# Gates and branch projections with rows stationary, and merged rows transposed for the output projection

## The chip, the core and the metric

The kernel runs on one core of a Trainium2 chip. The core has a matrix engine (TensorE, PE in the profile; its weight loads are PEld), a vector engine (VectorE, DVE), an activation engine (ScalarE, ACT), GpSimd (POOL), and SyncE (SP), which here issues the DMA transfers. SBUF is the working memory with 128 partitions; matmul results land in PSUM, which has eight banks of 128 x 512 float32 here. The metric is the device time of one execution in microseconds; lower is better.

A matmul has a stationary operand (loaded into the array as weights, 128 x 128 here) and a moving operand (128 x N columns that stream through it). The result has the stationary operand's columns on the partitions and the moving operand's columns along the row.

## The reference, cut to what matters

Two layers. Each has a token-mixing sub-layer with two attention branches, merged by gates, and then an MLP. The sequence has 256 rows, the model width is 1024.

```python
for l in range(DEPTH):
    ada = c_act @ w_ada[l] + b_ada[l]
    sh1, sc1, gt1, sh2, sc2, gt2 = [a[:, None, :] for a in jnp.split(ada, 6, axis=-1)]
    h = rms(x, g_mix[l]) * (1.0 + sc1) + sh1
    parts = jnp.split(h @ w_in[l], IN_SPLITS, axis=-1)
...
    y_a = gqa_attention(qa, ka, va) @ w_branch_a[l]
...
    y_b = dilated_attention(qs, kss, vs) @ w_branch_b[l]
    gate_a = jax.nn.sigmoid(parts[3 + 3 * N_B])
    gate_b = jax.nn.sigmoid(parts[4 + 3 * N_B])
    mixed = gate_a * y_a + gate_b * y_b
    x = x + gt1 * (mixed @ w_out[l])
    h2 = rms(x, g_mlp[l]) * (1.0 + sc2) + sh2
    x = x + gt2 * (jnp.square(jax.nn.relu(h2 @ w_ff1[l])) @ w_ff2[l])
```

The change concerns `gate_a`, `gate_b`, `y_a`, `y_b` (the two branch projections) and `mixed`.

## The kernel before, in words

**Precision.** Every large matmul is done with operands split in two: `hi` is the value rounded to the matmul's float32 form and `lo` the remainder. `mm3` issues three matmuls into the same PSUM accumulation: hi x hi, lo x hi, hi x lo. Weights arrive from HBM as 128 x 1024 float32 tiles of 512 KB into one of six `wr` buffers; ACT copies the tile to `hi`, DVE subtracts to get `lo` (`split_next`, called through `weights` and `weights_k`). These two operations are the groups `w<-wr` of ACT and `w<-wr,w` of DVE.

**Layouts.** The normalised rows `h` are kept transposed: `hT` has the model width on partitions (8 tiles of 128) and the 256 rows along the free axis, as hi and lo. Attention outputs `oa` (4 tiles) and `ob` (2 tiles) are kept in the same way.

**Two ways of multiplying.** The q, k, v chunks (`qkv_chunk`) use a piece of `hT` (128 of its rows) as the stationary operand and move 512 weight columns: the result has rows on partitions. The gates, the projection of branch A (`ya`) and of branch B (the loop at the end of `mixer`, called yb below) go the other way, through `wide`: 128 weight columns are stationary and all 256 rows move, so that the result has model columns on partitions and rows along the free axis, one 128 x 256 half of a PSUM bank at a time. A unit of each fills one bank.

- `gates(l, hT, G, u, bank)`, eight units a layer: two weight tiles, 2 x 8 x 3 matmuls of 256 columns, then on ACT a tanh out of PSUM into `G` and a scale-and-shift in place (a sigmoid). `G[0]` is gate A, `G[1]` gate B.
- `ya`, four units: one weight tile, 2 x 4 x 3 matmuls, then one DVE multiply of the bank by gate A into `M`.
- yb, four units: 2 x 2 x 3 matmuls, a DVE multiply by gate B, a DVE add of `M`, then ACT copies the sum to `mT` hi and DVE subtracts for `mT` lo.

`mT` is therefore already transposed (model width on partitions), as the output projection needs it for its stationary operand. The output projection takes each of the two blocks of 128 rows (t = 0, 1) against 512 columns of `w_out` at a time: 2 x 2 x 8 x 3 matmuls. Its result goes through `residual` and `make_h` into the MLP. In the MLP `two_sums` multiplies with weights stationary and both halves of `h2` moving: one matmul of 512 and one of 256 columns per weight tile's block.

**Order.** Every operation is recorded by a helper (all have line 551 in the profile) and a planner decides the order on each engine before anything is issued: `Plan.run` is a list scheduler over the engines with costs of its own and due times, run four times (`PASSES`) with the best kept; the tiles of a pool get buffers in that order. The recorded sequence within a mixer is written by hand in `CFG["seq0"]` and `CFG["seq1"]`: `c3` a qkv chunk, `u` or `v` a gate unit, `a` a step of attention A, `b` a pair of heads of attention B, `y` a unit of `ya`, `w` one step of ada (a 512 KB tile of `w_ada` multiplied by the conditioning vector and summed along the row on DVE: the group `s2k<-wr,c_act`). PSUM tiles all come from one pool of eight banks (`pa`, `pb` and `pt` are the same).

Attention A's step: scores of two heads, maximum on DVE, exponentials on ACT, scaling by the reciprocal sum on ACT, transposes of the probabilities by TensorE, a copy to SBUF on ACT, and the product with v. Attention B's pair does the same on 128 x 512 tiles, with a masked pass on DVE in place of the maximum.

## Time and profile before

| | |
|---|---|
| device time, median of 3 runs | 755.84 us |
| lowest and highest run | 755.43 and 757.5 us |
| span of the profiled execution, first to last instruction | 754.0 us |
| TensorE busy | 739.9 us, 98% |
| TensorE weight loads busy | 629.9 us, 84% |
| VectorE busy | 595.4 us, 79% |
| ScalarE busy | 470.7 us, 62% |
| moved by DMA | 180.47 MB, mean 239 GB/s |

The profile is one execution. A row of a timeline gives start, length, engine, line, operation, the tiles written and read with their shapes, and a count; in brackets the idle time of the engine before it and what ended it. A row of a group gives the same shapes with a count, and behind the bars the busy time in us and the mean of one in ns, then the idle time before it. Tile names: `ps` a PSUM bank, `w` a split weight tile, `wr` a raw one, `s2k` a small work tile, `consts` the identity of the transposes, `pr` probabilities, `qk` and `ka` queries and keys, `st` the softmax statistics.

In layer 0 the mixer's gates and attention lie between about 66 and 171 us of the span, yb from 171.57, the output projection from 177.23, and the MLP's first matmul at 199.95. In layer 1 the mixer runs from about 386 us, yb starts at 538.22 and the output projection at 543.87.

### The profile page before, as it was taken

What the parts mean: (1) busy time and instruction counts of PE and PEld (TensorE: products, weight loads), DVE (VectorE), ACT (ScalarE), POOL (GpSimd) and SP (SyncE); (2) the same over time, 40 slices, a digit from 0 to 9 for tenths busy, and PEclk for the clock granted to TensorE, in tenths of its full rate; (3) what the DMA queues carried; (4) which work ended last, traced back from release to release, by engine and by line L of the source; (5) the groups of instructions that cost most, each with busy time, mean ns of one, the idle gap of its engine ahead of it and who ended that gap; (6) DMA issues with size and microseconds to landing.
All of it is one profiled execution on the core that took longest, in us unless ns stands there. A gap on an engine that the chain in (4) does not pass through costs nothing.

```text
span 754.0 us, 11447 instructions
## 1 busy us (share of the span) xinstructions
PE 739.9 (98%) x4246; PEld 629.9 (84%) x4246; DVE 595.4 (79%) x905; ACT 470.7 (62%) x784; POOL 70.2 (9%) x60
## 2 busy tenths in 40 slices
PE   7999999999999999999999999999998999999997
PEld 4888898998788888888888788889987888888886
DVE  5999999889899989566499899778879976556633
ACT  8668469785558766655256557599535865555630
POOL 0007840000000060000002111000000000000000
PEclk9999999999999999999999999999999999999999
DMA  8996379976579999666145566966635986656201
GB/s 336 385 401 208 128 246 330 356 261 234 178 283 370 386 355 341 248 223 222 58 155 182 219 242 236 363 198 212 235 140 184 344 305 224 204 191 219 88 29 56
DMA packets 50391, 180.47 MB, mean 239 GB/s; under 512 B 5624, under 2 KB 6048, under 8 KB 50336
## 3 DMA queue, kind: packets, MB, share of 16 engines
q1 hardware_dynamic: 50336, 179.75, 66.6%
q8 instruction: 33, 0.54, 0.3%
q14 instruction: 22, 0.18, 0.1%
HBM read 178.66 MB, written 1.06 MB: 238 GB/s over the span
## 4 chain that ended last, share of the span: by engine, by line
PE 84%; DVE 7%; issue 4%; ACT 3%; DMA 1%; POOL 1%; SPq 0%; POOLq 0%; ACTq 0%; DVEq 0%
PE ps L551 84%; DVE s2k L551 4%; DVE w L551 2%; ACT s2k L551 2%; DVE rstd L551 1%; DMA x<-in_x 1%; ACT pr L551 1%; ACT w L551 0%; POOL s2k L551 0%; DVE x L551 0%; DVE hT L551 0%; ACT xT L551 0%; SPq L551 0%; POOL ss L551 0%; ACT c_act L551 0%
## 5 line engine op out<-in xcount | busy, mean ns | idle before, releaser
L551 DVE TENSOR_TENSOR w<-wr,w 128x1024 fp32r<-128x1024 f32 x236 | 288.0, 1238 | 61.0 <-ACT w L551 60.6
L551 ACT ACTIVATE w<-wr 128x1024 fp32r<-128x1024 f32 x236 | 245.6, 1058 | 87.2 <-PE ps L551 48.0
L551 PE MATMUL ps<-hT,w 128*128 128x256 f32 (+1 forms) x1664 | 263.8, 315 | 0.0
L551 PEld LDWEIGHTS ps<-hT,w 128*128 128x128 f32 x1664 | 234.4, 190 | 23.6 <-issue 2.6
L551 PE MATMUL ps<-w,r2k 128*128 128x512 f32 (+1 forms) x792 | 178.8, 385 | 0.0
L551 PEld LDWEIGHTS ps<-w,r2k 128*128 128x128 f32 x792 | 144.4, 188 | 30.1
L551 PE MATMUL ps<-w,hT 128*128 128x512 f32 x672 | 163.3, 399 | 5.0 <-DVE hT L551 2.7
L551 PEld LDWEIGHTS ps<-w,hT 128*128 128x128 f32 x672 | 126.2, 191 | 33.8 <-DVE hT L551 4.5
L551 DVE CUSTOM_DVE_ANT_0 s2k<-wr,c_act 128x1024 bf16<-128x1024 f32 x96 | 117.7, 1240 | 2.3 <-DMA wr<-in_w_ada 1.6
L551 ACT ACTIVATE s2k<-ps 128x512 f32<-128x512 f32 (+3 forms) x136 | 61.5, 479 | 64.0 <-PE ps L551 55.0
L551 PE MATMUL ps<-w,mT 128*128 128x512 f32 x192 | 44.5, 391 | 0.0
L551 ACT ACTIVATE s2k<-s2k 128x512 f32<-128x512 f32 (+1 forms) x62 | 38.3, 620 | 6.0 <-DVE s2k L551 5.2
L551 PEld LDWEIGHTS ps<-w,mT 128*128 128x128 f32 x192 | 35.8, 188 | 7.3
L551 POOL TENSOR_TENSOR rstd<-rstd,half 128x8 f32<-128x8 f32 (+1 forms) x20 | 35.7, 1795 | 61.7 <-DVE rstd L551 61.7
L551 DVE TENSOR_TENSOR s2k<-ps,s2k 128x256 f32<-128x256 f32 x56 | 23.6, 421 | 17.1 <-ACT s2k L551 17.1
L551 ACT ACTIVATE pr<-pr,st 128x256 f32<-128x256 f32 (+1 forms) x64 | 35.7, 614 | 0.6 <-DVE st L551 0.6
L551 POOL TENSOR_TENSOR ss<-ss,half 128x1 f32<-128x1 f32 x8 | 4.4, 554 | 312.2 <-DVE ss L551 312.2
L551 DVE TENSOR_TENSOR r2k<-s2k,r2k 128x512 fp32r<-128x512 f32 x28 | 19.6, 699 | 15.6 <-ACT r2k L551 15.6
L551 ACT ACTIVATE s2k<-x 128x512 bf16<-128x512 f32 x16 | 10.0, 627 | 31.2 <-DVE x L551 28.3
L551 DVE TENSOR_TENSOR s2k<-ps,gtb 128x512 f32<-128x512 f32 (+1 forms) x18 | 11.8, 659 | 20.5 <-PE ps L551 18.7
L551 PE MATMUL ps<-oa,w 128*128 128x256 f32 x192 | 26.1, 288 | 0.0
L551 PE MATMUL ps<-consts,s2k 128*128 128x128 f32 x148 | 22.6, 281 | 2.9 <-DVE s2k L551 2.4
(82 smaller groups left out, 498.1 us busy)
## 6 DMA issues: line engine op xcount, KB each, us to landing
wr<-in_w_ff SPq DMA_DIRECT2D x120, 512.0 KB, 5.2
wr<-in_w_ada SPq DMA_DIRECT2D x96, 512.0 KB, 5.3
wr<-in_w_gate SPq DMA_DIRECT2D x32, 512.0 KB, 5.1
wr<-in_w_qkv SPq DMA_DIRECT2D x24, 512.0 KB, 4.6
wr<-in_w_x SPq DMA_DIRECT2D x16, 512.0 KB, 3.2
wr<-in_w_out SPq DMA_DIRECT2D x16, 512.0 KB, 5.4
wr<-in_w_y SPq DMA_DIRECT2D x8, 512.0 KB, 5.5
wr<-in_w_ba SPq DMA_DIRECT2D x8, 512.0 KB, 4.9
```

Source lines behind the costliest of these rows:

```text
L551: getattr(self.real[o["e"]], o["op"])(*map(real, o["a"]), **{n: real(z) for n, z in o["k"].items()})
```

## The change

The gates and `ya` now work as the qkv chunks do: 128 rows of `hT` or `oa` are stationary and 512 weight columns move. Two PSUM banks, one for each block of rows, are filled by four weight tiles (a gate group, two of the old units) or two (`ya`). `G` and `M` have rows on partitions. The gate weights and those of branch A are laid out on the host in tiles that fit (`w_gate`, `w_ba`); sizes and counts of the tiles stay.

yb too has rows stationary. Its merged result has rows on partitions, and TensorE transposes it, four 128 x 128 blocks into one PSUM bank, from which ACT and DVE make `mT` hi and lo for one block of rows. The loop goes over the blocks of rows first, then over the two column halves; both weight tiles of branch B are fetched ahead of it. `CFG`, with the two hand-written sequences, is unchanged; `u`, `v`, `y`, `z` no longer name a bank.

```diff
-    def gates(l, hT, G, u, bank):
-        if u % 4 == 0:
-            G.append(tl("sbuf", [P, 2048], F32, "b8", NB8, f"G{l}{u}"))
-        ps = bank(f"g{l}_{u}")
-        for i in range(2):
-            wh, wl = weights_k(KT)
-            wide(ps, i, wh, wl, hT, KT)
-
-        z = G[u // 4][:, (u % 4) * 512 : (u % 4 + 1) * 512]
-        act.activation(z, ps, AF.Tanh, scale=0.5)
-        act.activation(z, z, AF.Copy, scale=0.5, bias=0.5)
+    def gates(l, hT, G, pss, u):
+        g, part = divmod(u, 2)
+        if g % 2 == 0 and part == 0:
+            G.append(tl("sbuf", [P, 2, D], F32, "b8", NB8, f"G{l}{g}"))
+        if part == 0:
+            pss[:] = [pb(f"g{l}_{g}_{t}") for t in range(2)]
+        for j in (2 * part, 2 * part + 1):
+            wh, wl = weights_k(2)
+            for t in range(2):
+                for k in range(2):
+                    kk = 2 * j + k
+                    lh, ll = hT.parts(kk, slice(t * P, (t + 1) * P))
+                    mm3(pss[t], lh, ll, wh[:, k, :], wl[:, k, :], kk == 0, kk == KT - 1)
+        if part == 0:
+            return
+        for t in range(2):
+            z = G[g // 2][:, t, (g % 2) * 512 : (g % 2 + 1) * 512]
+            act.activation(z, pss[t], AF.Tanh, scale=0.5)
+            act.activation(z, z, AF.Copy, scale=0.5, bias=0.5)
...
-        def ya(u, bank):
-            wh, wl = weights_k(4)
-            ps = bank(f"ya{l}_{u}")
-            for i in range(2):
-                wide(ps, i, wh[:, :, i * P : (i + 1) * P], wl[:, :, i * P : (i + 1) * P], T["oa"], 4)
-            dve.tensor_tensor(
-                fl(M[:, 2 * u : 2 * u + 2, :]), ps, G[0][:, u * 512 : (u + 1) * 512], op=ALU.mult
-            )
+        def ya(y):
+            c, part = divmod(y, 2)
+            if part == 0:
+                yps[:] = [pa(f"ya{l}_{c}_{t}") for t in range(2)]
+            wh, wl = weights_k(2)
+            for t in range(2):
+                for k in range(2):
+                    kk = 2 * part + k
+                    lh, ll = T["oa"].parts(kk, slice(t * P, (t + 1) * P))
+                    mm3(yps[t], lh, ll, wh[:, k, :], wl[:, k, :], kk == 0, kk == 3)
+            if part == 1:
+                cs = slice(c * 512, (c + 1) * 512)
+                for t in range(2):
+                    dve.tensor_tensor(M[:, t, cs], yps[t], G[0][:, t, cs], op=ALU.mult)
...
-        for v in range(2):
-            wh, wl = weights_k(2)
-            for uu in range(2):
-                u = 2 * v + uu
-                ps = pa(f"yb{l}_{u}")
-                for i in range(2):
-                    n0 = (2 * uu + i) * P
-                    wide(ps, i, wh[:, :, n0 : n0 + P], wl[:, :, n0 : n0 + P], T["ob"], 2)
-                t = s2k(f"yb{l}_{u}s")
-                dve.tensor_tensor(t, ps, G[1][:, u * 512 : (u + 1) * 512], op=ALU.mult)
-                dve.tensor_tensor(t, t, fl(M[:, 2 * u : 2 * u + 2, :]), op=ALU.add)
-                hi, lo = (fl(z[:, 2 * u : 2 * u + 2, :]) for z in mT)
-                act.activation(hi, t, AF.Copy)
-                dve.tensor_tensor(lo, t, f32(hi), op=ALU.subtract)
+        wb = [weights_k(2) for _ in range(2)]
+        for t in range(2):
+            ts = slice(t * P, (t + 1) * P)
+            for c in range(2):
+                cs = slice(c * 512, (c + 1) * 512)
+                ps = pa(f"yb{l}_{t}{c}")
+                for k in range(2):
+                    lh, ll = T["ob"].parts(k, ts)
+                    mm3(ps, lh, ll, wb[c][0][:, k, :], wb[c][1][:, k, :], k == 0, k == 1)
+                m = s2k(f"yb{l}_{t}{c}s")
+                dve.tensor_tensor(m, ps, G[1][:, t, cs], op=ALU.mult)
+                dve.tensor_tensor(m, m, M[:, t, cs], op=ALU.add)
+                tp = pt(f"mT{l}_{t}{c}")
+                for k in range(4):
+                    pe.transpose(tp[:, k * P : (k + 1) * P], m[:, k * P : (k + 1) * P], ident)
+                tv = tp.rearrange("p (k n) -> p k n", k=4)
+                hi, lo = (z[:, 4 * c : 4 * c + 4, ts] for z in mT)
+                act.activation(hi, tv, AF.Copy)
+                dve.tensor_tensor(lo, tv, f32(hi), op=ALU.subtract)
...
-    r["w_gate"] = tiles(blocks(wi[:, :, GA:], P), 1, 8).reshape(2, 16, P, 1024)
+    r["w_gate"] = tiles(blocks(wi[:, :, GA:], 512), 4, 2).reshape(2, 16, P, 1024)
...
-    r["w_ba"] = tiles(blocks(wa, 256), 1, 4).reshape(2, 4, P, 1024)
+    r["w_ba"] = tiles(blocks(wa, 512), 2, 2).reshape(2, 4, P, 1024)
```

More of the change, by code (lines that the diff above doesn't have):

```diff
@@ L1086, in mixer @@
         mT = []
-        def ya(u, bank):
-            wh, wl = weights_k(4)
-            ps = bank(f"ya{l}_{u}")
-            for i in range(2):
-                wide(ps, i, wh[:, :, i * P : (i + 1) * P], wl[:, :, i * P : (i + 1) * P], T["oa"], 4)
-            dve.tensor_tensor(
-                fl(M[:, 2 * u : 2 * u + 2, :]), ps, G[0][:, u * 512 : (u + 1) * 512], op=ALU.mult
-            )
-        M = tl("sbuf", [P, KT, S], F32, "b8", NB8, f"M{l}")
+        def ya(y):
[12 more added lines that the diff above has]
+                    dve.tensor_tensor(M[:, t, cs], yps[t], G[0][:, t, cs], op=ALU.mult)
+        gps, yps = [], []
+        M = tl("sbuf", [P, 2, D], F32, "b8", NB8, f"M{l}")
         for j in seq:
@@ L1101, in mixer @@
             elif j in "uv":
-                gates(l, hT, G, u, pa if j == "u" else pb)
+                gates(l, hT, G, gps, u)
                 u += 1
@@ L1110, in mixer @@
             elif j in "yz":
-                ya(y, pa if j == "z" else pb)
+                ya(y)
                 y += 1
```

## The prediction

> **What bounds the kernel now.** First the head of the page, then its chain of work that ended last, then the stretches in which only one kind of matmul runs, then the busy time of each engine over each mixer.
>
> ```profile
> span 754.0 us, 11447 instructions
> PE 739.9 (98%) x4246; PEld 629.9 (84%) x4246; DVE 595.4 (79%) x905; ACT 470.7 (62%) x784; POOL 70.2 (9%) x60
> PEclk9999999999999999999999999999999999999999
> PE 84%; DVE 7%; issue 4%; ACT 3%; DMA 1%; POOL 1%; SPq 0%; POOLq 0%; ACTq 0%; DVEq 0%
> ```
>
> TensorE is busy in 98% of the span, at the full granted clock in every slice, and carries 84% of the chain. So a change pays by what it takes off the time that TensorE needs, and costs by every wait that it puts on TensorE. The busy time of one matmul overlaps that of the next, so I price matmuls by their pitch: first start of one group to first start of the next, over the count. The timeline of TensorE (start, length, what, count) has pure stretches:
>
> ```profile
> 162.93 5.92 PE L551 MATMUL ps<-hT,w 128*128 128x256 f32 x48
> 168.69 3.04 PE L551 MATMUL ps<-oa,w 128*128 128x256 f32 x24
> 171.57 5.82 PE L551 MATMUL ps<-ob,w 128*128 128x256 f32 x48
> 177.23 15.84 PE L551 MATMUL ps<-w,mT 128*128 128x512 f32 x69
> 192.91 1.03 PE L551 MATMUL ps<-consts,s2k 128*128 128x128 f32 x8
> 193.70 6.42 PE L551 MATMUL ps<-w,mT 128*128 128x512 f32 x27
> ...
> 443.97 11.11 PE L551 MATMUL ps<-w,hT 128*128 128x512 f32 x48
> 454.91 4.83 PE L551 MATMUL ps<-hT,w 128*128 128x256 f32 x39
> ```
>
> Weights stationary, 256 columns moving: gates (168.69 - 162.93)/48 = 120 ns, ya (171.57 - 168.69)/24 = 120 ns, yb (177.23 - 171.57)/48 = 118 ns. Rows stationary, 512 weight columns moving, the form that the change goes over to: (454.91 - 443.97)/48 = 228 ns for qkv, (192.91 - 177.23)/69 = 227 ns in the output projection. Two of the old do the work of one new: 240 against 228 ns.
>
> **Part 1, fewer and wider matmuls.** Per layer the old gates are 8 units x 2 x 8 x 3 = 384 matmuls of 256 columns, ya 96, yb 48; the new ones are half as many of 512. The groups by shape confirm it for ya and yb:
>
> ```profile
> L551 PE MATMUL ps<-hT,w 128*128 128x256 f32 x1216 | 230.2, 285 | 0.0
> L551 PE MATMUL ps<-oa,w 128*128 128x256 f32 x192 | 26.1, 288 | 0.0
> L551 PE MATMUL ps<-ob,w 128*128 128x256 f32 x96 | 11.6, 279 | 0.0
> L551 PE MATMUL ps<-hT,w 128*128 128x512 f32 x448 | 157.3, 394 | 0.0
> ```
>
> (Of the 1216, 448 belong to the MLP's two_sums, one for each of its 448 wide matmuls; 768 are gates.) Both layers: 960 x 120 + 96 x 118 = 126.5 us before, 528 x 228 = 120.4 us after: -6.1 us. Bounds: with the output projection's 227 ns it is -6.7; if the wide form in the gates ran no better per column than the narrow one, 240 ns, it is nothing. I take -6.1, since the nearest row has the same hT as stationary operand and weights moving.
>
> A sentence apart: the Trainium skill, "TensorE: Matmul & The Clock Gate", section "Back-to-back issue gap", gives an isolated warm gap of N / 2.4 + 2.5 ns, so 109 and 216 ns for 256 and 512 columns. By it a pair saves only 2.5 ns, 528 pairs 1.3 us, and that speaks against the change. The rows have 120 and 228, so the trace does not agree and I keep its 12 ns.
>
> **Part 2, the transposes that come in.** yb now lands with rows on partitions, so four 128x512 results per layer are each turned by four 128x128 transposes: 8 groups in all. The trace has the same groups of four inside gate matmuls:
>
> ```profile
> 99.83 5.17 PE L551 MATMUL ps<-hT,w 128*128 128x256 f32 x41
> 104.84 0.61 PE L551 MATMUL ps<-consts,s2k 128*128 128x128 f32 x4
> 105.21 5.76 PE L551 MATMUL ps<-hT,w 128*128 128x256 f32 x46
> ```
>
> The four take 105.21 - 104.84 = 0.37 us to the next start, and the 41 before them 5.01 us instead of 41 x 0.120 = 4.92, 0.09 more: 0.46 us a group, 3.7 us in all. The eight at 192.91 take 0.79 us with no such step, 0.40 a group, 3.2 us. I take 3.6 us. The sum so far is -6.1 + 3.6 = -2.5 us.
>
> **Part 3, the seam from yb to the output projection.** DVE does as many operations as before (multiply, add, and the subtraction for lo, each four times a layer), ACT the same four copies; both now read the transpose from PSUM.
>
> ```profile
> L551 DVE TENSOR_TENSOR s2k<-ps,G 128x512 f32<-128x512 f32 x8 | 5.5, 688 | 0.9 <-PE ps L551 0.9
> L551 DVE TENSOR_TENSOR s2k<-s2k,M 128x512 f32<-128x512 f32 x8 | 5.4, 689 | 0.1
> L551 ACT ACTIVATE mT<-s2k 128x512 fp32r<-128x512 f32 x8 | 5.0, 628 | 9.9 <-DVE s2k L551 9.9
> L551 DVE TENSOR_TENSOR w<-wr,w 128x1024 fp32r<-128x1024 f32 x236 | 288.0, 1238 | 61.0 <-ACT w L551 60.6
> ```
>
> Count from the first yb matmul. The first group of six ends at 6 x 0.228 = 1.4 us, plus about 0.2 for its end; multiply and add finish at 3.0. In the order of the changed kernel 15 matmuls stand ahead of the first transposes: 3.4 us, no wait. hi ends at 4.7, lo at 5.4, and the first matmul on mT is due after 24 matmuls and 8 transposes, at 6.4: covered by the other yb groups. The other half of the rows (t = 1) is needed only after the 48 matmuls of t = 0, 11 us later. The tight place is the last transpose of layer 0: on DVE, w_183's split stands between its multiply and its add, so the add ends at 7.5 + 1.24 + 0.7 = 9.4 and TensorE is there at 9.2. Behind it the whole output projection is queued; I count 0.3 us. In layer 1 the splits are ahead of it, and the same count leaves no wait. Bounds 0 and 1.2 (one more split in the way). No transfer moves: the two re-laid weight tensors arrive in the same number of 512 KB tiles.
>
> **Part 4, what the shorter matmuls were covering.** DVE is almost as full as TensorE in the mixer of layer 0, and ACT during attention B. Busy time by stretch (layer 0's mixer, its attention B, its output projection, layer 1's mixer):
>
> ```profile
> core 0: us, PE busy (x) PEld busy (x) DVE busy (x) ACT busy (x) POOL busy (x), PEclk, DMA share, GB/s
> 66.30:171.50 105.20, 104.02 (x812) 92.86 (x811) 97.56 (x164) 80.47 (x161) 32.04 (x23) 1.00 0.75 261
> 405.70:538.20 132.50, 130.93 (x928) 114.95 (x927) 110.70 (x188) 94.16 (x174) 12.57 (x8) 1.00 0.71 252
> ...
> 142.00:163.00 21.00, 21.00 (x203) 18.85 (x202) 18.63 (x44) 20.06 (x39) 0.00 (x0) 1.00 0.78 276
> 177.20:200.00 22.80, 22.80 (x107) 18.92 (x106) 21.80 (x33) 10.23 (x19) 0.56 (x1) 1.00 0.55 185
> ```
>
> In layer 0's mixer TensorE falls by 240 pairs x 12 ns = 2.9 us, to 101.1, against 97.6 of DVE, whose work stays. That is 3.5 us of room, and in attention B ACT has 20.06 of 21.00. The new form also keeps two PSUM banks open (one for each half of the rows) over four weight tiles of gates or two of ya, where the old kept one open over two or one; there are eight banks. In the changed order the second pair of heads of attention B starts its scores only after the first pair's last product with v; before, they stood in between (142.06 and 147.07 against 153.41):
>
> ```profile
> 142.06 2.02 PE L551 MATMUL ps<-qk 64*128 64x256 f32 x24
> ...
> 147.07 1.15 PE L551 MATMUL ps<-qk 64*128 64x256 f32 x12
> ...
> 153.41 1.96 PE L551 MATMUL ps<-s2k,v 128*64 128x256 f32 x24
> ```
>
> ```profile
> 143.99 0.72 ACT L551 ACTIVATE pr<-pr,st 128x512 f32<-128x512 f32 x1 [0.56 <-DVE st L551]
> ...
> 146.12 2.55 ACT L551 ACTIVATE pr<-pr,st 128x512 f32<-128x512 f32 x4
> ```
>
> ```profile
> L551 DVE CUSTOM_DVE_ANT_0 s2k<-wr,c_act 128x1024 bf16<-128x1024 f32 x96 | 117.7, 1240 | 2.3 <-DMA wr<-in_w_ada 1.6
> ...
> L551 DVE CUSTOM_DVE_ANT_0 pr<-ps,mask 128x512 f32<-128x512 f32 x16 | 10.4, 685 | 3.0 <-PE ps L551 2.8
> ```
>
> So the second pair's first transpose waits for its scores, a mask pass of 0.69 us that stands behind an ada product of 1.24 on DVE, two exponentials of 0.72 and a scaling of 0.64, with nine wide matmuls (2.1 us) as cover: about 2 us of wait. Counted through operation by operation with these durations, the stretch from the first score to yb comes to 28.9 us. Before it took 171.57 - 142.06 = 29.5, from which part 1 takes 72 pairs x 12 ns = 0.9. So 0.3 us of the wait is a net loss. Attention A of this layer is rearranged in the same way; I give it 0.9, three of its transposes left with 0.3 us each. Together +1.2 for layer 0, and nothing for layer 1, where DVE has 22 us of room. Bounds: nothing, and the 2.9 us of layer 0's gain with the 2 us on top, 4.9. A gain is excluded: no operation of DVE or ACT goes.
>
> **Sum.** -6.1 + 3.6 + 0.3 + 1.2 = -1.0 us on the span of 754.0: 753.0. The page has no time for the profiled execution but the span; the span lies 1.84 us below the median of the runs, 755.84, which I take for launch and end and leave as it is: 754.8 us. A difference under 0.3%, 2.3 us, cannot be told from no change here. So the forecast is "the same", a little to the fast side.
>
> **Rivals.**
>
> *All of it arrives (faster, chance 0.28).* No wait of parts 3 and 4 comes, and the row-wise gates, which need one half of the rows at a time, also fill gaps at the head of layer 1, where narrow gates needed both halves:
>
> ```profile
> 398.62 0.73 PE L551 MATMUL ps<-consts,s2k 128*128 128x128 f32 x5 [0.60 <-DVE s2k L551]
> ...
> 410.58 0.66 PE L551 MATMUL ps<-consts,s2k 128*128 128x128 f32 x4 [0.44 <-DVE s2k L551]
> ```
>
> Those are 0.60 + 0.44 = 1.0 us. -2.5 - 1.0 = -3.5: 752.3 us. For it: layer 1 has room on all engines. Against it: DVE at 93% in layer 0's mixer.
>
> *PSUM banks set attention (slower, chance 0.20).* Open two-bank groups push the score matmuls back in both layers. A pair of heads then needs its chain in series: a mask pass 0.69, four exponentials 2.9, four scalings 2.5, four copies out of PSUM 2.4, some 9 us with the splits between, while TensorE has 7 us of its own and filler work. 2.4 us twice, and about 1.2 a layer for attention A, is 7.2 us: -2.5 + 7.2 = +4.7, 760.5 us. It decides from 4.8 us of new waits on. For it: the banks, and the order named above. Against it: the planner has four passes to place filler, and layer 1 keeps more gates for it.
>
> *No cheaper per column (slower, chance 0.05).* Wide gate matmuls cost 240 ns, as two narrow ones: +3.6 + 1.5 = +5.1, 760.9 us. The qkv row at 228 stands against it. By the skill's gap formula above it would be 1.3 better than that.
>
> **How the numbers follow.** Forecast 0.47, faster rival 0.28, the two slow ones 0.20 and 0.05: faster 0.28, same 0.47, slower 0.25. The forecast's own bounds are -6.1 + 3.2 = -2.9, 752.9 us, and -6.1 + 3.7 + 1.2 + 4.9 = +3.7, 759.5 us. The range goes a little past both: down to 751.5, toward the faster rival with 227 ns in part 1 (0.6) and the lesser price of the transposes (0.4), up to 759.8. The slow rivals end beyond it, at 760.5 and 760.9, but part of their waits would end within; less than 2 in 10 is left out.
>
> **What would show it.** Right: gates, ya and yb matmuls 128x512 at 227 to 230 ns pitch; eight new groups of transposes at 0.4 to 0.5 us; from the first yb matmul to the first of the MLP about 1.6 to 2 us longer in each layer, 106 to 172 us of layer 0 shorter by 1 to 2. Wrong: waits of TensorE for ACT pr or DVE s2k of over 5 us more in total (the PSUM rival), or a wide pitch above 235 ns.

## The result and the profile after

| | before | after |
|---|---|---|
| device time, median (19 runs each) | 755.8 us | 758.4 us |
| lowest and highest | 754.44 to 759.26 | 755.87 to 760.23 |
| span of the profiled execution | 754.0 us | 757.2 us |

The ratio after to before is 1.003, 95% interval 1.0019 to 1.0041: some 2.3 us slower, right on the bound under which a difference, as the prediction has it, "cannot be told from no change here". The time lies in the predicted range (751.5 to 759.8), but on the other side of the kernel before: 758.4 against a forecast of 754.8.

First the head of the page of the changed kernel: span, busy time of each engine, TensorE's granted clock in 40 slices, and the shares of the chain that ended last.

```profile
span 757.2 us, 10461 instructions
PE 739.1 (98%) x3750; PEld 599.7 (79%) x3750; DVE 596.6 (79%) x905; ACT 471.6 (62%) x784; POOL 68.6 (9%) x60
PEclk9999999999999999999999999999999999999999
PE 72%; DVE 11%; ACT 7%; issue 5%; DMA 4%; SPq 0%; POOL 0%; POOLq 0%; DVEq 0%; ACTq 0%
```

TensorE's instructions fell from 4246 to 3750 (528 narrow ones out net, 32 transposes in), and the other engines have the counts of before. TensorE's busy time fell by only 0.8 us while the span grew by 3.2, so in this pair of profiles its idle time grew by 4.0 us, from 14.1 to 18.1 (span less busy time). Its share of the chain fell from 84% to 72%, in favour of DVE, ACT and DMA; 12% of the span is 90 us, so that shift is no price, only a sign that other engines now end more of the waits. The groups of the new shapes:

```profile
L551 PE MATMUL ps<-w,hT 128*128 128x512 f32 x1056 | 261.6, 399 | 5.5 <-DVE hT L551 2.9 <-ACT hT L551 2.3 <-ACT v L551 0.2
L551 PE MATMUL ps<-w,oa 128*128 128x512 f32 x96 | 25.1, 401 | 1.3 <-DVE st L551 1.3
```

The gates are now inside the first group (1056 = 672 + 384). The pitch is read from the timeline of TensorE (start, length, what, count, and in brackets the idle time before it with what ended it), here in the second half of layer 1's mixer:

```profile
470.95 11.85 PE L551 MATMUL ps<-w,hT 128*128 128x512 f32 x51
482.74 1.57 PE L551 MATMUL ps<-ka,qk 64*128 64x256 f32 x12
...
525.33 5.73 PE L551 MATMUL ps<-w,hT 128*128 128x512 f32 x24
530.90 8.32 PE L551 MATMUL ps<-w,oa 128*128 128x512 f32 x36
539.06 1.33 PE L551 MATMUL ps<-w,ob 128*128 128x512 f32 x5
```

(482.74 - 470.95)/51 = 231 ns, (530.90 - 525.33)/24 = 232 and (539.06 - 530.90)/36 = 227 ns: the predicted 228, a little more in the gates. The seam of layer 0, from yb to the MLP:

```profile
170.61 3.67 PE L551 MATMUL ps<-w,ob 128*128 128x512 f32 x15
174.12 0.60 PE L551 MATMUL ps<-consts,s2k 128*128 128x128 f32 x4
174.47 0.95 PE L551 MATMUL ps<-w,ob 128*128 128x512 f32 x3
175.25 0.60 PE L551 MATMUL ps<-consts,s2k 128*128 128x128 f32 x4
175.61 1.64 PE L551 MATMUL ps<-w,ob 128*128 128x512 f32 x6
177.09 0.63 PE L551 MATMUL ps<-w,mT 128*128 128x512 f32 x2
177.56 0.60 PE L551 MATMUL ps<-consts,s2k 128*128 128x128 f32 x4
177.91 2.09 PE L551 MATMUL ps<-w,mT 128*128 128x512 f32 x8
179.84 0.61 PE L551 MATMUL ps<-consts,s2k 128*128 128x128 f32 x4
...
200.77 0.62 PE L551 MATMUL ps<-w,hT 128*128 128x512 f32 x2
```

No row carries a bracket: TensorE does not wait here. From the first yb matmul to the MLP it takes 200.77 - 170.61 = 30.16 us, 1.78 more than before. Now the two halves of layer 1's mixer, split at the first scores of attention (`ps<-ka,qk`), before and then after (stretch, length, then each engine's busy time and count, the granted clock, the share of DMA and GB/s):

```profile
386.46:462.18 75.72, 73.61 (x407) 62.70 (x407) 68.36 (x119) 42.53 (x66) 15.04 (x10) 1.00 0.60 214
462.18:538.22 76.04, 75.98 (x610) 67.67 (x610) 60.12 (x103) 60.51 (x126) 0.00 (x0) 1.00 0.77 269
```

```profile
387.23:462.95 75.72, 72.74 (x335) 58.20 (x335) 68.29 (x118) 42.32 (x66) 15.12 (x10) 1.00 0.60 215
462.95:539.06 76.11, 74.86 (x442) 57.44 (x441) 60.32 (x103) 61.61 (x126) 0.00 (x0) 1.00 0.78 271
```

In the first half TensorE has 0.87 us less work, just what its three gate units (72 pairs x 12 ns) should give, and the half is as long as before: TensorE idles 2.98 us instead of 2.11. In the second half there are 168 pairs by the counts (610 - 442), so 2.0 us were due; its busy time fell by only 1.12 us, and it idles 1.25 us instead of 0.06. Some of those idle times by their rows, two of the first half and both of the second:

```profile
399.38 0.74 PE L551 MATMUL ps<-consts,s2k 128*128 128x128 f32 x5 [0.60 <-DVE s2k L551]
...
429.45 0.63 PE L551 MATMUL ps<-consts,s2k 128*128 128x128 f32 x4 [0.52 <-DVE s2k L551]
...
510.32 1.20 PE L551 MATMUL ps<-w,oa 128*128 128x512 f32 x4 [0.80 <-DVE st L551]
512.89 0.66 PE L551 MATMUL ps<-consts,pr 128*128 128x128 f32 x4 [0.45 <-ACT s2k L551]
```

At the head of the layer TensorE waits for the rotated queries and keys, which DVE and ACT make at their own pace; coming earlier only lengthens the wait. In before, after and the kernels e1 to e10 of the next section this half takes 75.3 to 76.1 us, whichever form its matmuls have, and also with DVE lightened (e5 76.01, e6 75.36). In attention B a ya matmul waits for an operation on `st`, and a transpose of probabilities for a copy `s2k`. Neither is an input of the waiting instruction (ya reads `oa` and `w`, the transpose reads `pr`). What DVE and ACT did just then, from their timelines:

```profile
508.44 1.21 DVE L551 CUSTOM_DVE_ANT_0 s2k<-wr,c_act 128x1024 bf16<-128x1024 f32 x1
...
509.57 0.69 DVE L551 CUSTOM_DVE_ANT_0 pr<-ps,mask 128x512 f32<-128x512 f32 x1
510.19 0.08 DVE L551 DVE_READ_ACCUMULATOR2_ANT st<- 128x1 f32 x1
```

```profile
512.24 0.60 ACT L551 ACTIVATE s2k<-ps 128x512 f32<-128x512 f32 x1
```

DVE reads scores out of a PSUM bank for the mask until 510.26, behind an ada product of 1.21 us, and ya goes on at 510.32; ACT copies a bank out until 512.8, and the transposes start at 512.89. The only kind of tile that each pair of instructions has in common is `ps`, so TensorE waits for a bank to come free; the trace gives the banks no numbers, and that is inferred. In the old form no such wait stood in this half.

All stages, from the same rows in each kernel, stand in the table of the next section.

### The profile page after: what moved, and what is told of

It is laid out like the page before. It is cut to its first block, busy times and chain, and to the rows that moved or that the text cites. A ratio compares the mean times of both kernels' runs of the same rounds, so it can differ in the third digit from the quotient of the medians.

```text
span 757.2 us, 10461 instructions
## 1 busy us (share of the span) xinstructions
PE 739.1 (98%) x3750; PEld 599.7 (79%) x3750; DVE 596.6 (79%) x905; ACT 471.6 (62%) x784; POOL 68.6 (9%) x60
## 4 chain that ended last, share of the span: by engine, by line
PE 72%; DVE 11%; ACT 7%; issue 5%; DMA 4%; SPq 0%; POOL 0%; POOLq 0%; DVEq 0%; ACTq 0%
PE ps L551 72%; DVE s2k L551 6%; DVE w L551 4%; ACT s2k L551 2%; DMA wr<-in_w_qkv 2%; ACT w L551 2%; ACT pr L551 2%; DMA wr<-in_w_x 1%; DMA x<-in_x 1%; DVE rstd L551 1%; DVE hT L551 0%; DVE x L551 0%; DVE st L551 0%; ACT xT L551 0%; DVE pr L551 0%
## 5 line engine op out<-in xcount | busy, mean ns | idle before, releaser
L551 PE MATMUL ps<-w,hT 128*128 128x512 f32 x1056 | 261.6, 399 | 5.5 <-DVE hT L551 2.9
L551 PEld LDWEIGHTS ps<-w,hT 128*128 128x128 f32 x1056 | 194.5, 189 | 52.1 <-DVE hT L551 5.4
L551 PE MATMUL ps<-hT,w 128*128 128x512 f32 (+1 forms) x896 | 160.3, 339 | 0.0
L551 PEld LDWEIGHTS ps<-hT,w 128*128 128x128 f32 x896 | 138.1, 188 | 20.8
L551 PEld LDWEIGHTS ps<-consts,s2k 128*128 128x128 f32 x180 | 20.9, 142 | 12.0 <-DVE s2k L551 5.1
L551 PE MATMUL ps<-consts,s2k 128*128 128x128 f32 x180 | 26.9, 279 | 3.4 <-DVE s2k L551 2.5
```

Source lines behind the costliest of these rows:

```text
L551: getattr(self.real[o["e"]], o["op"])(*map(real, o["a"]), **{n: real(z) for n, z in o["k"].items()})
```

## The experiments

The stages are cut on TensorE's timeline: the start (to the first transposes after the opening, 66.30 before), layer 0's mixer (to the first yb matmul), its seam (to the first MLP matmul), its MLP (to the eight transposes at layer 1's head), layer 1's mixer and seam, and the rest. Each column is the difference to before in us, from one profiled execution; the ratio is of five rounds of runs against before, with its 95% interval.

| kernel | start | mixer 0 | seam 0 | MLP 0 | mixer 1 | seam 1 | rest | ratio |
|---|---|---|---|---|---|---|---|---|
| before (us) | 66.30 | 105.27 | 28.38 | 186.51 | 151.76 | 28.34 | 187.44 | |
| after | +1.07 | -2.03 | +1.78 | -0.05 | +0.07 | +1.79 | +0.57 | 1.003 [1.0019, 1.0041] |
| e1 gates only | -0.68 | +1.88 | +0.32 | +0.53 | -0.33 | +0.06 | -1.08 | 1.0043 [1.0029, 1.0057] |
| e2 ya only | +0.08 | -1.25 | 0.00 | +0.58 | -0.38 | +0.04 | +0.53 | 0.9999 [0.9988, 1.0010] |
| e3 seam only | +0.60 | +0.08 | +2.74 | -0.06 | 0.00 | +1.75 | -1.61 | 1.0043 [1.0028, 1.0059] |
| e4 no transposes | +0.53 | -2.03 | +0.12 | +0.19 | -0.06 | -0.02 | -1.03 | 0.9989 [0.9975, 1.0003] |
| e5 before, DVE light | +1.28 | -1.13 | +0.01 | +0.72 | +0.70 | +0.84 | -0.02 | 1.0006 [0.9994, 1.0018] |
| e6 after, DVE light | +0.51 | -2.40 | +1.75 | +0.20 | -0.35 | +1.81 | +0.58 | 0.9997 [0.9984, 1.0010] |
| e7 narrow, two banks | +0.64 | -0.21 | +0.04 | +0.04 | +1.35 | +0.06 | -1.12 | 1.0012 [0.9996, 1.0029] |
| e8 wide, ya one bank | +0.92 | -1.63 | +1.84 | +0.21 | -1.45 | +1.75 | -1.24 | 1.0008 [0.9997, 1.0019] |
| e9 before, 7 banks | +1.25 | -1.05 | 0.00 | 0.00 | +0.47 | +0.62 | +0.51 | 1.0021 [1.0010, 1.0032] |
| e10 after, 7 banks | +0.98 | -0.83 | +1.79 | +0.15 | +0.33 | +1.82 | -1.04 | 1.0065 [1.0047, 1.0082] |
| e11 all on one bank | -0.46 | +6.20 | +1.75 | +2.34 | -1.93 | +2.05 | +0.45 | 1.0098 [1.0079, 1.0118] |
| e12 e8, new order | +0.56 | -4.05 | +1.89 | +0.06 | -0.95 | +1.78 | +0.11 | 0.9995 [0.9981, 1.0009] |
| e13 before, new order | +3.91 | -3.50 | 0.00 | +0.33 | -0.03 | +0.01 | -2.92 | 0.9974 [0.9961, 0.9987] |
| e14 after, new order | -0.04 | -1.63 | +1.87 | +0.15 | -0.37 | +1.74 | +0.58 | 1.0036 [1.0020, 1.0051] |
| e15 e12, other tail | +0.52 | -4.33 | +1.89 | +0.04 | +0.65 | +1.74 | +0.09 | 0.9984 [0.9968, 0.9999] |
| e16 before, other tail | +1.51 | +0.05 | 0.00 | +0.16 | +0.02 | +0.01 | -2.95 | 0.9978 [0.9966, 0.9990] |

Start and rest swing by 1 to 1.5 us whatever the edit (e1 to e12 leave the rest's code alone and have -1.6 to +0.6 there); the reason for the rest is in the last section. So the mixers and seams are compared by stage, and a kernel as a whole by its ratio. What the difference of before and after in mixers and seams adds up to, -2.03 + 1.78 + 0.07 + 1.79 = +1.6 us, agrees with the ratio's 1.4 to 3.1.

**The parts one by one.** Taken from the changed kernel by putting the old code back in the other places:

```diff
 e1: gates as after; ya, yb and the seam as before
 e2: ya as after; gates, yb and the seam as before
 e3: yb, transposes and the seam as after; gates and ya as before
 e4: all as after, but
-                tp = pt(f"mT{l}_{t}{c}")
-                for k in range(4):
-                    pe.transpose(tp[:, k * P : (k + 1) * P], m[:, k * P : (k + 1) * P], ident)
-                tv = tp.rearrange("p (k n) -> p k n", k=4)
+                tv = m.rearrange("p (k n) -> p k n", k=4)
```

> Only the gates go over to stationary rows and 512 moving columns; ya, yb and the output projection stay as before (no transposes). The gate values land in another order than ya and yb expect, so the output is another one. TensorE arithmetic from the pitches of before and after: 768 x 0.120 - 384 x 0.230 = 3.8 us less. Theory 'cover' (DVE and the weight supply pace much of the mixers, so that part of a shorter matmul comes back as a wait): about half arrives, 1 to 3 us faster than before. Theory 'banks' (two PSUM banks held open push attention back): the gates hold most of the bank time, so it gives back nearly all of it, -1 to +1 us. If the wide form were no cheaper: no gain and no new waits.

> Only ya goes over to stationary rows (values in another order than its gate, so the output is another one). Arithmetic: 192 x 0.120 - 96 x 0.227 = 1.2 us less. 'Cover': 0 to 1 us faster, layer 1's share with it. 'Banks': ya is open while attention B needs its banks, in both layers, so 0.5 to 2 us slower than before, with waits of TensorE for DVE st or ACT s2k in attention B.

> Only yb goes over to stationary rows, with the 32 transposes behind it; gates and ya stay narrow (values in another order, so the output is another one). Both theories: the seam from the first yb matmul to the MLP is 1.8 us longer per layer than before (28.4 and 28.3 us), the total +3 to +4 us, no change elsewhere beyond the planner's reshuffling of about 1 us. If the transposes were hidden by waits that were there anyway: under +1 us.

> The changed kernel with its 32 transposes left out: hi and lo are taken from the merged rows in SBUF as they are, untransposed (so the output is another one). If the transposes' TensorE time is what the seam costs: 3.2 to 3.7 us less than the changed kernel, 1 to 2 us faster than the kernel before, and a seam of about 28.3 us in each layer. If the seam is set by the DVE and ACT chain: at most 1 us less than the changed kernel.

The seams settle themselves. Where the transposes are (after, e3) a seam is 1.75 to 1.79 us longer, and 2.74 once (e3, layer 0, with 0.79 us of wait for DVE `s2k` before the MLP's own eight transposes); without them (e4) it is back within 0.12. e4's seam on TensorE:

```profile
170.07 5.76 PE L551 MATMUL ps<-w,ob 128*128 128x512 f32 x24
175.67 16.48 PE L551 MATMUL ps<-w,mT 128*128 128x512 f32 x71
```

So the eight groups cost (30.16 - 28.50) + (30.13 - 28.32) = 3.47 us, 0.43 a group. The wide yb gives nothing: (175.67 - 170.07) = 5.60 us for 24, where 48 narrow ones took 5.66. e4 as a whole is at 0.9989, some 3 us below the changed kernel; against before, the interval reaches just past no change.

e1 is a miss for adding up the parts. The gates alone made layer 0's mixer 1.88 us longer and ya alone made it 1.25 shorter, where 192 and 48 pairs should give -2.3 and -0.6. Each variant is laid out anew by the planner, and a layout alone can move a mixer by more than the terms in question (e12 below: 2.4 us against e8, with the same matmuls). A single part's ratio is therefore no price of that part. For banks the two say this: in layer 1's second half neither has a wait for one (idle time 0.08 us in e1, 0.06 in e2), though ya alone had been expected to bring such waits. There it takes the gates and ya together.

**Is it VectorE's load?** The prediction had put the lost cover on DVE (97.6 of 105 us in layer 0's mixer). In both kernels the ada products of the mixers were cut to 64 of their 1024 columns:

```diff
-        dve.tensor_tensor_reduce(junk, raw, c_act, 0.5, 0.0, ALU.mult, ALU.add, col)
+        n = 64 if few[0] else 1024
+        dve.tensor_tensor_reduce(junk[:, :n], raw[:, :n], c_act[:, :n], 0.5, 0.0, ALU.mult, ALU.add, col)
```

> The kernel before, with the ada products inside both mixers (one DVE pass of 1.24 us each) taken over 64 of their 1024 columns, so that some 1.1 us of DVE work goes with each and the transfers stay; the output is another one. It is the base for the next run. If DVE paces parts of the mixers (layer 0: 97.6 of 105.3 us busy, first half of layer 1's: 66.0 of 73.3), it is 1 to 5 us faster than before; if TensorE alone does, under 1 us.

> The changed kernel with the same ada products over 64 of 1024 columns. Theory 'cover' (layer 1's mixer does not take the shorter matmuls because DVE paces its first half): with DVE unloaded the gates and ya bring their arithmetic in layer 1 too, layer 1's mixer is 2 to 3 us shorter than in the light kernel before, and this kernel is 0 to 2 us faster than that one. Theory 'banks': the waits in attention B stay, layer 1's mixer is as long as in the light kernel before or longer, and this kernel is 1.5 to 3 us slower than it.

In layer 0's mixer DVE fell by 20 us, after first and then the lightened one:

```profile
67.37:170.61 103.24, 101.83 (x572) 78.40 (x571) 96.28 (x163) 79.43 (x160) 30.41 (x23) 1.00 0.75 263
```

```profile
66.81:169.68 102.87, 101.85 (x572) 77.80 (x571) 76.27 (x165) 81.23 (x162) 28.68 (x23) 1.00 0.79 276
```

The stretch got 0.37 us shorter, and layer 1's mixer went from +0.07 to -0.35: 0.8 us by stage. By the ratio the changed kernel gains more, from 1.003 to 0.9997, 2.5 us; the two profiled executions don't show where the rest lies. The kernel before gains nothing from the same relief (1.0006). So 20 us of DVE work are no bound for the old form, and the new one gets some of its price back. Neither side's forecast came: layer 1's mixer is 1.0 us shorter than in e5, where 'cover' asked for 2 to 3, and the kernel is not slower than e5, as 'banks' had asked. In layer 1's second half the waits fall from 1.25 to 0.60 us, yet the half is as long as in after (76.05 us against 76.11). That DVE frees banks late because ada products stand before the reads, as in the row at 508.44, is thus a reading of the rows; no run shows it as the price.

**Is it the PSUM banks?** Three ways to ask: hold two banks with the old narrow matmuls (e7), hold one at a time for ya with the wide ones (e8), and take one bank away from the mixers of either kernel by parking a result in it (e9, e10).

```diff
 e7, from before: two units share their weights' order, each of two banks open over both
+        if u % 2 == 0:
+            gps[:] = [pb(f"g{l}_{u}_{b}") for b in range(2)]
+        for ps in gps:
             wh, wl = weights_k(KT)
-            wide(ps, i, wh, wl, hT, KT)
+            wide(ps, u % 2, wh, wl, hT, KT)
... (ya likewise)
 e8, from after: both weight tiles first, then one bank per block of rows
+            yps.append(weights_k(2))
             if part == 0:
-                yps[:] = [pa(f"ya{l}_{c}_{t}") for t in range(2)]
+                return
+            w2 = [yps.pop(0) for _ in range(2)]
...
             for t in range(2):
+                ps = pa(f"ya{l}_{c}_{t}")
...
 e9, e10: a bank taken at the head of each mixer, read at its end
+        hog = pt(f"hog{l}")
+        pe.transpose(hog[:, :P], T["qa"][:, 3, P : 2 * P], ident)
...
+        dve.tensor_tensor(s2k(f"hog{l}s")[:, :P], hog[:, :P], ob, op=ALU.mult)
```

> The kernel before (narrow matmuls, no transposes), with gates and ya filling two PSUM banks in turn over the same number of weight tiles as the changed kernel does, instead of one; the same matmuls and the right output. Only the time that banks are held grows. 'Banks': 1 to 3 us slower than before, with new waits of TensorE for DVE st or ACT s2k in attention B of either layer. 'Cover': within 1 us of before.

> The changed kernel with ya working through one block of rows and then the other, so that each of its banks is open for 12 matmuls instead of 24 (both weight tiles are held instead); right output. 'Banks': the two waits for DVE st ahead of ya (0.54 us in layer 0 and 0.80 us in layer 1) go, 1 to 2 us faster than the changed kernel. 'Cover': within 1 us of it.

> The kernel before with one PSUM bank taken away from each mixer: a transpose of queries fills it once attention's queries are ready, and one small DVE multiply frees it when attention B's output is done (one transpose and one DVE operation of 0.3 us a layer added, the product is not used). Theory 'banks': attention B sits on the edge with eight banks even before, so 1 to 2 us slower, most of it in layer 1's mixer, as when gates and ya held two banks. 'Cover': within 0.7 us of before.

> The changed kernel with the same bank taken away. 'Banks': it needs more of them at once, so the bank costs it at least what it costs the kernel before: 1 to 4 us slower than the changed kernel, 3.5 to 6 us slower than before, with longer waits for DVE st and ACT s2k in attention B. 'Cover': within 0.7 us of the changed kernel.

With the old matmuls and the new hold, layer 1's mixer is 1.35 us longer than before, 1.04 of it in the second half (e7; that half in the columns used above, then from TensorE's timeline a gate matmul that waits for a copy that it does not read):

```profile
463.00:540.08 77.08, 76.52 (x609) 67.63 (x609) 60.20 (x102) 60.88 (x126) 0.00 (x0) 1.00 0.77 268
...
513.39 1.45 PE L551 MATMUL ps<-hT,w 128*128 128x256 f32 x10 [0.55 <-ACT s2k L551]
```

With the new matmuls and one bank for ya it is 1.52 us shorter than after (-1.45 against +0.07), 1.14 of it in the second half, where TensorE's idle time is gone (e8; first column the stretch, then its length and PE's busy time):

```profile
463.14:538.11 74.97, 74.97 (x441) 57.42 (x441) 59.40 (x103) 61.26 (x126) 0.00 (x0) 1.00 0.76 257
```

The two ask the same from opposite sides and agree: a second open bank is worth 1.0 to 1.1 us of layer 1's second half (in e7 of gates and ya, in e8 of ya alone). Where its code and banks are the same, this half repeats within 0.02 us (76.04, 76.04 and 76.03 in before, e3 and e16; 76.11 and 76.10 in after and e4), so both differences are clear of scatter. The waits at the layer's head stay (0.60, 0.49, two of 0.41 and three of 0.3 us in e8). Layer 0 does not follow: e8's wait ahead of ya is gone there, but one of 1.48 us for ACT `pr` comes at 146.45, and that mixer is 0.40 us longer than after's. As whole kernels e7 and e8 can't be told from before (1.0012 and 1.0008).

One bank less costs before 1.6 us (ratio 1.0021) and after 2.6 us (1.0065 against 1.003), with the added transpose and DVE operation of each layer in it; the intervals don't tell these two prices apart. The traces don't place them in attention B: in layer 1's second half e9 has no wait for a bank (idle time 0.06 us, as before), and e10 one of 0.69 us where after has 0.80 and 0.45. That a bank is short in both kernels thus rests on the ratios alone.

If a bank is what is missing, gates on one bank too should pay. e11 fetches all four weight tiles of a gate group before the first matmul and fills one bank after the other:

```diff
-        for j in (2 * part, 2 * part + 1):
-            wh, wl = weights_k(2)
+        gws.extend(weights_k(2) for _ in range(2))
...
         for t in range(2):
+            ps = pb(f"g{l}_{g}_{t}")
+            for kk in range(KT):
+                wh, wl = gws[kk // 2]
```

> ya as in the run with one bank at a time, and the gates too: a group takes its four weight tiles, then fills the bank of one block of rows and then the other, so that a bank is open for 24 matmuls of 5.5 us instead of 48. The output is right. The price is three more split weight tiles held in the 14 SBUF buffers, which leaves no room to split ahead. If banks are all that was wrong: 1 to 2 us faster than the run with ya alone. If SBUF takes the place of PSUM as the scarce store: slower than that run, by 1 to 5 us, with waits of TensorE for DVE w or ACT w in the mixers.

It is the slowest kernel of all, 1.0098, and the profiled execution is the longest of its six (760.68 to 766.23 us). Layer 1's mixer is the shortest of all (-1.93), which fits with banks having been in the way there. But layer 0's mixer is 6.2 us longer. TensorE idles 4.5 us in it instead of 1.2, most of all before attention A's probabilities, and the mean granted clock is 0.97: two stretches of 3.41 us, from 90.7 and 124.9 us, run at half clock, which is some 3.4 us (more on this in the last section). First the mixer, then that wait:

```profile
65.84:177.31 111.47, 106.95 (x579) 81.83 (x580) 102.12 (x168) 84.45 (x164) 30.35 (x24) 0.97 0.75 258
...
124.21 1.54 PE L551 MATMUL ps<-consts,pr 128*128 128x128 f32 x8 [2.56 <-ACT pr L551]
```

A likely reason for the waits is that weight tiles which stand split in SBUF until their group is complete hold back the tiles behind them, so that filler runs out. No run tests it, and of the expected waits for split weights only one of 0.47 us shows in the mixers.

**Is it the order?** The two lists of units were made for narrow units. For the changed kernel with e8's edit another order was sought, and likewise for before; e14 is the changed kernel itself with e12's lists.

```diff
 e12 (from e8) and e14 (from after)
-  seq0="c3 w a v w c4 w w u w u u w a w a w w w w w w v a w w v v w w w b w y w w w b w y w y v y"
-  seq1="w u c2 w c3 u w c4 w u w w w a c5 w u a w w a w w v w b w v a b w w y w w v v w w w y y w w y"
+  seq0="c3 w a v c4 w w w u u u a w w w a w w w w w w v a w w v v w w w b w y b y w w w w w y v y"
+  seq1="c2 w u u c3 w c4 w w u w w a a c5 w u w w a w v w b w v a w w y w b w v v w w y y w y w"
 and in layer 0's MLP
-  ada_f0=[5, 5, 0, 5, 3, 5, 0, 1, 1]
+  ada_f0=[5, 6, 0, 4, 3, 5, 1, 1, 2]
 e13 (from before)
+  ada_f0=[5, 4, 0, 5, 3, 5, 0, 1, 1], ada_f1=[2, 0, 2, 0, 3, 1, 0, 0, 0]
+  seq0="w a v c3 w c4 w u w u w a w a w u w w w w w w v a w w v v w w w b w y w w w w y b w y v y"
+  seq1="w u c2 w w c3 w u c4 w u w w w a c5 w u a w w a w w v w b w v a b w w y w w v v w w w y y w w y"
```

> Changed kernel with ya on one PSUM bank at a time and, on top, another hand order of the units (places of c, u, v, w, a, b, y in both lists and of 3 ada units in the MLP). Theory 'order': layer 1's mixer did not gain because the lists were laid out for units of narrow matmuls; with another order the waits for the rotations at its head shrink from 2.8 to under 1.5 us and at least one mixer gets 1.5 to 3 us shorter than with ya on one bank in the old order (103.64 and 150.31): span 751 to 753 by the same start and tail, ratio to before 0.995 to 0.999. Rival 'the rotations and the heads pace it whatever the order': mixers within 1 us of those, ratio 0.999 to 1.003.

> The kernel before with its lists re-ordered in the same way, no other edit: what an order alone is worth without the change. Theory 'order was fit for the narrow form': nothing to win here, ratio 0.998 to 1.002, both mixers within 1 us of 105.27 and 151.76. Rival 'any order can be bettered': the ratio falls as much as that of the changed kernel falls from its own old order, 0.995 to 0.998, and what the re-ordered changed kernel wins says nothing for the change.

> The changed kernel as it is (ya holds two banks) with the same lists as the re-ordered one on one bank. If order and bank are separate terms, it is 1.4 to 2.5 us slower than that one, by waits in attention B for DVE st or ACT pr as in the changed kernel's layer 1 (0.80 + 0.45 us): ratio 0.998 to 1.002. If the order alone was at fault, it is within 0.7 us of it.

In e12 TensorE has no idle time in layer 0's mixer at all, which is 4.05 us shorter than before:

```profile
66.86:168.08 101.22, 101.22 (x572) 78.20 (x571) 96.75 (x162) 80.49 (x162) 29.54 (x22) 1.00 0.78 273
```

Layer 1's mixer did not follow (-0.95 against e8's -1.45). One wait for the rotations grew to 1.96 us, where they were expected to shrink: for that layer the "rotations pace it" side was right. Mixers and seams sum to -4.05 + 1.89 - 0.95 + 1.78 = -1.3 us; the ratio of 0.9995 can't be told from none and lies on the rival's side (0.999 to 1.003). e14, with two banks, is at 1.0036: its mixers are 2.42 and 0.58 us longer than e12's, so the kernel with two banks is the slower one under this order too, by 3.1 us by the ratios, more than the 1.4 to 2.5 expected. But the expected waits in attention B are not there: layer 1's second half has no idle time, and mixer 0's waits are 1.12 and 0.66 us for rotations. How the second bank costs under this order stays open.

The surprise is e13. A new order for the kernel before wins more, 0.9974, where nothing was expected if its order was fit (the rival, that any order can be bettered, was right), and not in the mixers: start and mixer 0 together are 0.4 us longer, the win is in the rest. One of its edits is the list of ada units in layer 1's MLP. e15 and e16 put that list alone into e12 and into before:

```diff
-  ada_f1=[3, 0, 2, 0, 2, 0, 0, 1, 0]
+  ada_f1=[2, 0, 2, 0, 3, 1, 0, 0, 0]
```

> The re-ordered changed kernel on one PSUM bank (e12) with the list of ada units in layer 1's MLP of the re-ordered kernel before (2 0 2 0 3 1 0 0 0 in place of 3 0 2 0 2 0 0 1 0). Theory 'the change pays once waits are out of its way': the stretch after layer 1's MLP begins falls from 187.55 to 184.5-186 us, span 750.5 to 752, ratio 0.994 to 0.9975, at or under that of the re-ordered kernel before (0.9974). Rival 'the tail's gain of that kernel belongs to its earlier order': the stretch stays at 186 to 187.6, ratio 0.998 to 1.001.

> The kernel before with the same one list changed and nothing else. If the list carries the gain of the re-ordered kernel before: the stretch after layer 1's MLP begins falls from 187.44 to 184.5-186 us and the ratio is 0.996 to 0.999. If the gain came with the rest of its order: ratio 0.999 to 1.001.

e16 shows that the list alone does it: 0.9978, and the rest 2.95 us shorter. Before each MLP TensorE waits for `hT`; before first, then e16, where two more matmuls cover part of the wait:

```profile
572.55 0.95 PE L551 MATMUL ps<-w,hT 128*128 128x512 f32 x3
574.95 0.50 PE L551 MATMUL ps<-w,hT 128*128 128x512 f32 x1 [1.45 <-DVE hT L551]
```

```profile
573.41 1.39 PE L551 MATMUL ps<-w,hT 128*128 128x512 f32 x5
575.34 0.49 PE L551 MATMUL ps<-w,hT 128*128 128x512 f32 x1 [0.54 <-DVE hT L551]
```

In e15 the same list does not have that effect, the wait is 1.45 us and the rest stays long. So the kernels that beat both are before with this one list (0.9978) or with the whole new order (0.9974); the changed kernel with a new order, one bank for ya and the same list reaches 0.9984, and its interval overlaps theirs.

## Why the prediction went wrong, step by step

- **Part 1, the pitch: right in pure stretches** (227 to 232 ns). The size was too good: the gates read above run at 231 to 232, so a pair saves 8 to 9 ns there, and yb saved 0.06 us a layer instead of 0.2. In the mixers, where gates and ya stand between other work, TensorE's busy time fell by 2.2 us (layer 0), 0.87 and 1.12 us (the halves of layer 1), 4.2 us where 480 pairs make 5.8. By the Trainium skill's formula ("TensorE: Matmul & The Clock Gate", section "Back-to-back issue gap") a pair saves 2.5 ns. The pure stretches here keep 8 to 13, so the doubt of it was right.
- **The clock was misread, without effect on the sum.** A nine in the row `PEclk` is 90% or more, not the full clock: before itself runs 3.41 us at half clock from 575.71 (last section).
- **Part 2, the transposes: right.** 3.6 us predicted, 3.47 measured by taking them out (e4).
- **Part 3, the seam: right** as a sum. 1.78 and 1.79 us a layer, inside the 1.6 to 2 named. The 0.3 us of wait for layer 0's last transpose did not show: its row has no bracket.
- **Part 4 for layer 0: right in sum, by luck.** -2.9 + 1.2 = -1.7 predicted, -2.03 measured. The waits that were to make the 1.2 us, before transposes of probabilities, are not there. The two that are, 0.80 us before a product with v (124.56) and 0.54 before ya (155.49), stand in the place of before's own waits, and idle time grew only from 1.2 to 1.4 us; the rest is work that fell by 2.2 us instead of 2.9. The cause it gave, a DVE without room, shows little by stage: with 20 us less work on DVE the stretch gains 0.37 us (e6).
- **Part 4, "nothing for layer 1, where DVE has 22 us of room": this is the step that failed.** It kept the whole 2.9 us of 240 pairs; the mixer gained nothing (+0.07). It asked only whether an engine has room, and room over 132 us says nothing on waits. In the first half TensorE already waited for the rotations, and 0.87 us less work became 0.87 us more wait there; the five rows that showed it in the trace of before (0.60, 0.44, 0.26, 0.35 and 0.35 us) were partly quoted, under the faster rival, as gaps that wide gates would fill. They were the sign that the stretch is paced by something else. In the second half 1.19 us of new waits came, and the open banks took 1.0 to 1.1 us (e7, e8).
- What remains of layer 1 is about 0.9 us, by which TensorE's busy time in the second half fell short of the 2.0 us that were due. It is missing without any wait too: e8's second half is 1.07 us shorter than before's, not 2.0. The pitch of 231 to 232 ns instead of 228 in its five gate units would be 120 x 3.5 ns = 0.4 us of it, an estimate; no run tests that by itself, and it stays open.

By stage the miss is this: mixers and seams were to give -1.0 us and gave +1.6, and layer 1's mixer alone is 2.95 us of the difference. The two profiled executions differ by another 1.6 us in start and rest, where the code is the same, so the 3.2 us between the spans is not the price; the 2.3 us of the ratio is.

The slow rival had a right mechanism, PSUM banks held open, at a quarter of its price: it put 7.2 us on it, and TensorE's new waits in attention B are 0.54 us in layer 0 and 1.25 in layer 1. The wrong-side result needed no more, because the forecast's gain was only 1.0 us.

## What to carry to other kernels

Where TensorE already waits inside a stretch, less work for it ahead of the waits can be worth nothing, as in the first half of layer 1: subtract the expected gain from each such stretch before summing, however full TensorE is overall. Count how many PSUM banks a new loop order keeps open and for how long, and expect the price in whichever stage also needs banks; moving the hold into SBUF can cost more (e11). And before crediting a change, give the old kernel the same retuning: here one list of filler units took the kernel before to 0.9978, no worse than the changed kernel with all its retuning (0.9984).

## What the runs showed that was not expected

**A wait of 1.45 us can cost as much again.** In the 12 us after the wait for `hT` in layer 1 (row above) the mean granted clock was 0.86 in 10 of the 16 profiled kernels that have a wait of 1.45 us, and 1.00 in the other 6; with the wait cut to 0.54 us (e13, e16) it was 1.00 in both. In before:

```profile
574.95:586.95 12.00, 11.78 (x52) 9.72 (x53) 10.68 (x17) 6.12 (x12) 0.00 (x0) 0.86 0.63 221
```

The stage "rest" is 187.4 to 188.0 us with the drop and 185.8 to 186.4 without. That is why the same code scatters there, and the 40-slice row of the clock hides it. It is also about half of what e16 wins in that stage: its 184.5 us is 2.95 below before, which has the drop, and 1.3 to 1.9 below the kernels without one.

The clock falls to 0.50 for one stretch of 3.41 us, which makes the 12 us mean (12 - 3.41/2)/12 = 0.86. In a profile such stretches start whole multiples of 3.413 us apart (in before at 15.93, 575.71 and 753.20: 164 and 52 times), so the trace shows a fixed grid. What counts is how much idle time falls into one window of this grid. Behind the wait for `hT` stands a second one of 0.23 us; in before both lie in one window, in e1 the second falls into the next. Before, then e1, each with the window of the long wait and the one after it (columns as above; behind the busy times the granted clock):

```profile
572.30:575.71 3.41, 1.74 (x10) 0.94 (x8) 2.81 (x6) 2.64 (x7) 0.00 (x0) 1.00 0.69 247
575.71:579.12 3.41, 3.41 (x10) 2.83 (x11) 3.34 (x7) 1.84 (x4) 0.00 (x0) 0.50 0.04 17
```

```profile
573.69:577.10 3.41, 1.96 (x12) 1.23 (x10) 2.81 (x6) 2.31 (x6) 0.00 (x0) 1.00 0.74 226
577.10:580.51 3.41, 3.18 (x17) 2.59 (x17) 3.34 (x8) 2.87 (x5) 0.00 (x0) 1.00 0.18 72
```

Before idles 1.67 us of its window and the next one is at half clock; e1 idles 1.45 us and it is not. Over all 18 profiles, from 20 us to TensorE's last matmuls, every window with 1.67 us of idle time or more was followed by a drop (12 of 12), and of those with less two were, both in e11 (1.37 and 1.57 us); elsewhere up to 1.62 us passed without one. e12 and e15 lie on both sides of this: the same 1.96 us wait in layer 1's mixer, at 447 us, leaves 1.62 us in one window in e12 and all 1.96 in e15, the clock behind it is 1.00 and 0.86, and e15's mixer is 1.6 us longer. The Trainium skill, "TensorE: Matmul & The Clock Gate", section "Part 1: The HAM clock gate", says that the clock falls to half after an idle window of about 3.4 us and that this window runs freely, so that its phase varies from run to run. The traces agree with the window, the half rate and the varying phase; a whole idle window was not needed here, some half of one was enough.

**The layout of filler moves a mixer by 2 us and more.** e1's layer 0 (+1.88), whose own matmuls should have given -2.3, shows that parts of a planned kernel don't add.
